# A two-layer decoder trunk on one core: who sends the mixers' turned pieces, and when a few tied steps run

## The chip, the cores and the metric

The kernel runs on one core of one Trainium2 chip. A core has four engines that compute, each with its own stream of instructions in a fixed order: TensorE (PE in the profile, its weight loads PEld), VectorE (DVE), ScalarE (ACT) and GpSimd (POOL). SyncE (SP) only issues transfers. ScalarE and GpSimd issue transfers too. All transfers of the core run on 16 DMA engines, whoever issued them; an instruction waits for others through semaphores.

The metric is the time of the whole program on the device in microseconds (us), the median of several runs. The profile is one further execution, with every instruction and DMA packet recorded.

## The reference, cut to what matters

The input is one sequence of 256 positions with 2048 features, all float32. Two layers are applied to it:

```
h = rms_norm(x);  x = x + mixer(h);  h = rms_norm(x);  x = x + conv_ffn(h)
layer 0: mixer_ab (projection 2048 -> 6144 = u,v,q,f,i,g of 1024; output projection 2048 -> 2048)
layer 1: mixer_c  (projection 2048 -> 8208 = q,k,v,g of 2048 and 16 gate columns; output 2048 -> 2048)

mixer_ab, part A: u, v = gelu(u), gelu(v);  v = rms_norm(v) per head
                  mixed[t] = sum_s tril(sp_w)[t, s] v[s] + sp_b       # 8 heads, chunks of 128
                  y_a = u * mixed
          part B: f = lb + (1 - lb) sigmoid(f);  k = (1 - lb) sigmoid(-f_logit)
                  state = f * state + k v;  o = q state               # 8 heads, gated recurrence
                  y_b = rms_norm(o) * silu(g)
mixer_c: q, k = rms_norm per head;  c = cumsum(log_sigmoid(f + b_f))
         p = softmax(q k / sqrt(128) + c[t] - c[s], causal);  y = (p v) * sigmoid(g)     # 16 heads
conv_ffn: z = h @ w_up (2048 -> 11264); causal width-3 convolution; (silu(a) * b) @ w_down (5632 -> 2048)
```

`lb` comes from a softmax over `hgrn_gamma`; `1 - lb` is called the gate floor's complement here, `omlb` in the code.

## The kernel before, in words

**Weights.** Nearly all of the time is matrix products with weights that are read once from memory. A weight tile is 128 x 1024 float32 (512 KB), fetched by SyncE (`weights`, L196). Each product is made of three matmuls in a reduced format: ScalarE copies the tile to its high part `wh` (L207), VectorE subtracts to get the low part `wl` (L212), and TensorE multiplies wh and wl with the high part of the activations and wh with their low part (L268 to L270 with the tokens' columns in 512-wide blocks, L288 to L290 in blocks of four heads). One tile feeds 12 matmuls. There are four buffers for a fetched tile and three for each part, so ScalarE and VectorE can be up to three tiles ahead of TensorE.

**Steps.** Everything else is written as Python generators that are advanced once per weight tile: `tick()` is called just before each tile is fetched, and `after(n, g)` starts a generator n ticks later. That sets where an instruction stands in its engine's stream. `LAG` is 6 and `LAST` is 7. A helper can tie an instruction behind the latest weight work that was handed over: `sum_in` and `behind(..., "sub")` put a VectorE instruction behind the latest wl subtraction, `act_in` and `copy_in` a ScalarE instruction behind the latest wh copy, `mm_in` a matmul behind the latest of the main products. Instructions that are not tied are placed by the scheduler of the framework, which may put them earlier. `project_pair` runs two column blocks of an output projection in turns: 12 of 16 row tiles of the first, 8 of the second, then the rest of each.

**Turning.** A projection in the mixers leaves a piece of 128 x 1024 elements with tokens on the partitions; what follows wants features there. `transposed` (L305 to L316) has VectorE transpose 32 x 32 blocks into `tmp` (L308) and then issues 16 transfers of 32 KB that put the blocks in place (L314). Unless a caller says otherwise they alternate between SyncE and GpSimd, eight each, so SyncE's share stands in the same queue as the weight fetches. SyncE's transfers wait for `tmp` and hold up whatever is behind them there. The mixers turn 28 pieces: 12 in mixer AB and 16 in mixer C. Their readers stand `LAG` ticks later: `add_four` adds a piece of an output projection to the residual `x` (L159, by `sum_in`) and feeds the next norm, `gates` and `queries` read the f and q pieces of mixer AB, `gated` and `spatial` its g and u pieces, `attend` the q and k pieces of mixer C, and `gate` its g pieces. Both FFNs turn their pieces in the same way, in `four` and `add_y`.

**The start of mixer AB.** ScalarE's queue fetches constants late: the identity and masks, the spatial weights `wt[0]`, their bias `wt[1]`, the convolution's columns and the levels' masks `kst`. VectorE casts `kst` to `msk` (L480) and masks `wt[0]` (L481) untied, right where the fetches are issued in the program. `values` squares and sums the eight heads' v (L353 and L354 in `sumsq`), takes the reciprocal root and scales v (L498); `mix` multiplies them with the masked weights. Both run in `mixes`, six ticks after the v projection. Then `omlb`, 8 columns of 128 features, is written to a buffer `od` in device memory feature by feature (L543, by GpSimd) and read back on all partitions as `orow` (L544), which scales the keys (L676).

**The start of mixer C.** The forget gate's 16 columns ride along in `keys_gate`. `forget` makes the running sums `fc`, writes them to device memory (`cd`, L813) and fetches them on all partitions in four loads of four heads, 512 KB each (`rows`, L791, GpSimd), at ticks 0, 4, 8 and 12 behind. `attend` reads the tile `cb` so filled in L839 and L841, four heads per load.

Of the kernel before, what the change touches and what calls it, by code (L numbers as in the profile page):

```python
# [8 lines left out]
F32 = mybir.dt.float32  # L9
# [6 lines left out]
P = 128  # L16
# [38 lines left out]
def tile_trunk(ctx: ExitStack, tc: tile.TileContext, x, pp_d, cst_d, mlev_d, msk_d,  # L55
# [87 lines left out]
    def after(n, g):  # L143
        soon.append([n, g])
# [160 lines left out]
    def transposed(src, tmp, dst, queues=None):  # L305

        for T in range(2):
            V.transpose(tmp.rearrange("p (b m i t) -> p b m i t", b=4, m=4, t=2)[:, :, :, :, T],  # L308
                        src(T).rearrange("p (m b j) -> p b m j", m=4, b=4))
        n = 2 * BLK  # L310
        for a in range(4):
            for b in range(4):
                qs = queues or (nc.sync, nc.gpsimd)
                qs[(a + b) % len(qs)].dma_start(dst[BLK * b:BLK * (b + 1), :, a * n:(a + 1) * n],  # L314
                                  tmp[BLK * a:BLK * (a + 1), b * 4 * n:(b + 1) * 4 * n]
                                  .rearrange("p (m r) -> p m r", m=4))  # L316
# [83 lines left out]
    def add_four(q, ps, z, tmp, dst, nxt):  # L400
        for T in range(2):
            SC.activation(z[:, T], ps[T], AF.Copy)
        transposed(lambda T: z[:, T], tmp, dst)

        def rest():
            for i in range(4):
                m = 4 * q + i
                sum_in(xT[m], xT[m], dst[:, i], ALU.add)
                nxt.feed(m)
                if q < 3 or i % 2:  # L410
                    yield
            if q == 3:
                for _ in range(WAIT):
                    yield
                yield from nxt.finish_tok()

        after(LAST if q == 3 else LAG, rest())


    def mixer_ab(norm):  # L420
# [45 lines left out]
        def fetch_late(*args):  # L466
# [6 lines left out]
              for _ in range(2)]  # L473
# [3 lines left out]
        msk = hp.tile([P, NL * P], BF16, tag="msk", name="msk")  # L477
        kst = hp.tile([P, NL * P], F32, tag="smk", name="kst", bufs=1)
        fetch_late(kst, msk_d)
        V.tensor_copy(msk, kst)  # L480
        V.tensor_tensor(wt[0], wt[0], cst[:, K_TRI:K_TRI + P].unsqueeze(1)  # L481
                        .to_broadcast([P, NH, P]), ALU.mult)

        ss = hp.tile([P, LANE], F32, tag="ss", name="ss")

        def values():
            for g in range(2):
                for T in range(2):
                    i = (2 * g + T) * 4
                    j = hp.tile([P, 512], F32, tag="smk", name=nm("junk"), bufs=1)  # L490
                    sumsq(ss[:, i:i + 4], gv[g][:, T], j)
                    yield
            rsq(ss[:, 0:2 * NH], ss[:, 0:2 * NH], P)
            for g in range(2):
                for T in range(2):
                    i = (2 * g + T) * 4
                    v4 = gv[g][:, T].rearrange("p (h d) -> p h d", d=P)
                    V.tensor_tensor(v4, v4, ss[:, i:i + 4].unsqueeze(2).to_broadcast([P, 4, P]), ALU.mult)  # L498
                yield

        mg = [keep("mg") for _ in range(NH)]
# [16 lines left out]
                mix(h)  # L518
                yield

        after(6, mixes())


        gam = pp[:, C_GAM:C_GAM + 3 * NH]
# [15 lines left out]
        V.tensor_scalar(lb, lb, 2.0 ** -63, None, ALU.max)  # L540
        od = dp.tile([NH, P], F32, tag="od", name="od")
        orow = hp.tile([P, NH * P], F32, tag="orow", name="orow")
        nc.gpsimd.dma_start(od.rearrange("h p -> p h"), omlb)  # L543
        nc.gpsimd.dma_start(orow.rearrange("p (h d) -> p h d", d=P), od.partition_broadcast(P))  # L544
        dgc = hp.tile([P, LANE], F32, tag="dgc", name="dgc")[:, 0:2 * NH].rearrange("p (h t) -> p h t", t=2)

# [175 lines left out]
        def spatial(j, z):  # L722
            while left[0] or j and yB[4 * j - 1] is None:
                yield
            act_in(z, z, AF.Gelu)
            for i in range(4):
                b = 4 * j + i
                m = mg[b].rearrange("p (t n) -> p t n", t=2)
                V.tensor_tensor(m, m, natural(z[:, i]), ALU.mult)
                yB[b] = quad("ya")  # L730
                split(yB[b], mg[b], turn=True)
                yield
# [17 lines left out]
    def mixer_c(norm):  # L750
# [37 lines left out]
        cb = hp.tile([P, CH * S], F32, tag="big", name="cb").rearrange("p (h s) -> p h s", s=S)  # L788

        def rows(to, of):  # L790
            nc.gpsimd.dma_start(to, of)  # L791
            yield

        def forget():
            f, fa, fc, on = (hp.tile([P, S], F32, tag=t, name=t)[0:CH] for t in ("f", "fa", "fc", "on"))
            ft = hp.tile([P, 2, LANE], F32, tag="ft", name="ft")
            V.memset(on, 1.0)
            for T in range(2):
                SC.activation(ft[:, T, 0:CH], pa[T][:, 0:CH], AF.Copy, scale=Rt[:, T:T + 1])
            yield  # L800
            ps = bank()
            for T in range(2):
                turn_in(ps[0:CH, T * P:(T + 1) * P], ft[:, T, 0:CH], ident)
            behind(V.tensor_scalar(f, ps[0:CH, 0:S], pp[0:CH, C_BF:C_BF + 1], None, ALU.add), "sub")
            yield
            copy_in(fa, f, AF.Abs)
            act(fa, fa, AF.Exp, scale=-1.0)
            act(fa, fa, AF.Ln, bias=one1[0:CH])
            yield
            V.scalar_tensor_tensor(f, f, 0.0, fa, ALU.min, ALU.subtract)  # L810
            V.tensor_tensor_scan(fc, on, f, 0.0, ALU.mult, ALU.add)
            cd = dp.tile([CH, S], F32, tag="cd", name="cd")
            nc.gpsimd.dma_start(cd, fc)  # L813
            for g in range(4):
                c = slice(4 * g, 4 * g + 4)
                after(4 * g, rows(cb[:, c], cd[c].partition_broadcast(P)))
            yield
            ps = bank()
            for T in range(2):
                turn_in(ps[:, T * CH:(T + 1) * CH], fc[:, T * P:(T + 1) * P], ident[0:CH, 0:CH])  # L820
            V.tensor_copy(ct, ps[:, 0:2 * CH].rearrange("p (t c) -> p t c", t=2))
# [104 lines left out]
        def gate(q, z):  # L926
            while left[0] or gone[0] < q:
                yield
            for T in range(2):
                act(z[:, T], z[:, T], AF.Sigmoid)  # L930
                V.tensor_tensor(z[:, T], z[:, T], os_[q][:, T], ALU.mult)
            yield
            t = piece("turn", 4)
            transposed(lambda T: z[:, T], flat(piece("tmp", 2)), heads(t))
            gone[0] += 1
            for _ in range(LAG):
                yield
            for i in range(4):
                if not room:
                    tag, n = ("big", 8) if not yB else ("o", 2)  # L940
                    w = hp.tile([P, n * 512], F32R, tag=tag, name=nm("yc"), bufs=1 if n > 2 else CH // 4)
                    room.extend(w[:, c * 512:(c + 1) * 512] for c in range(n))
                y = room.pop(0)
                src = view(heads(t)[:, i], 0, (2, 2), (1, 2), (4, P // 2))
                h, lo = (y[:, i_ * S:(i_ + 1) * S].rearrange("p (t u n) -> p t u n", t=2, u=2) for i_ in range(2))
                copy_in(h, src, AF.Copy)
                V.tensor_tensor(lo, src, h.bitcast(F32), ALU.subtract)
                yB.append(y)
                yield

        gone = [0]
        for q in range(CH // 4):
# [12 lines left out]
    def ffn(l, norm, last):  # L965
# [11 lines left out]
        def four(j0, ps=None):  # L977
            ps = ps or project_four(w_up[l, j0:j0 + 4], A, KT)
            tmp, zt = room()

            def empty():
                while norm.Rt is None:
                    yield
                z = [hp.tile([P, 512], F32, tag="z", name=nm("z"), bufs=2) for _ in range(2)]
                for T in range(2):
                    SC.activation(z[T], ps[T], AF.Copy, scale=norm.Rt[:, T:T + 1])  # L986
                transposed(lambda T: z[T], tmp, zt)
                for _ in range(LAG):
                    yield

            return zt, empty()
# [44 lines left out]
        def add_y(q, finish):  # L1036
            tmp, zt = room()
            end = last and finish and q == 2
            transposed(lambda T: y[:, T, q * 512:(q + 1) * 512], tmp, zt,
                       (nc.sync, SC, nc.gpsimd) if end else None)  # L1040

            def rest():
                for i in range(4):
                    m = 4 * q + i
                    r = sum_in(xT[m], xT[m], zt[:, i], ALU.add)
                    if end:
                        deep["early"] = r
                        tc.add_manual_dep(r.ins, deep["sum"].ins.name, order, reason="after an earlier sum")
                    if finish:
                        finish_x(m)  # L1050
                    if (q < 3 or i % 2) and not end:
                        yield
                if q == 3 and not last:
                    for _ in range(WAIT):
                        yield
                    yield from nxt.finish_tok()

            after(2 if end else LAST if q == 3 else LAG, rest())
# [148 lines left out]
```

## Time and profile before

| | us |
|---|---|
| three runs | 2301.01, 2301.51, 2304.57 |
| median | 2301.51 |
| the profiled execution | 2308.89 |
| its span, first to last instruction | 2307.1 |
| TensorE busy | 2289.0 (99%) |
| VectorE busy | 1559.8 (68%) |
| ScalarE busy | 1313.3 (57%) |
| GpSimd busy | 358.3 (16%) |

The span has these stages: mixer AB up to about 400, the first FFN to about 1130, mixer C to about 1580 and the second FFN to the end. 434.85 MB were read from HBM. The queue of SyncE and ScalarE moved 451.97 MB, GpSimd's 23.69 MB.

A row of a timeline has the start in us from the first instruction, the duration, engine, line, operation, out<-in with shapes, and in brackets the idle time of the engine just before it with what ended it. A row of issues has what was moved, who issued it, how often, its size and the median time from issue to landing. Because TensorE is nearly always busy, the rows to look for are those in which it was not.

### The profile page before, as it was taken

What the parts mean: (1) busy time and instruction counts of PE and PEld (TensorE: products, weight loads), DVE (VectorE), ACT (ScalarE), POOL (GpSimd) and SP (SyncE); (2) the same over time, 40 slices, a digit from 0 to 9 for tenths busy, and PEclk for the clock granted to TensorE, in tenths of its full rate; (3) what the DMA queues carried; (4) which work ended last, traced back from release to release, by engine and by line L of the source; (5) the groups of instructions that cost most, each with busy time, mean ns of one, the idle gap of its engine ahead of it and who ended that gap; (6) DMA issues with size and microseconds to landing.
All of it is one profiled execution on the core that took longest, in us unless ns stands there. A gap on an engine that the chain in (4) does not pass through costs nothing.

```text
span 2307.1 us, 31430 instructions
## 1 busy us (share of the span) xinstructions
PE 2289.0 (99%) x10370; PEld 1899.5 (82%) x10370; DVE 1559.8 (68%) x2369; ACT 1313.3 (57%) x1955; POOL 358.3 (16%) x664
## 2 busy tenths in 40 slices
PE   9999999999999999999999999999999999999999
PEld 7788888888888888888878888878888888888887
DVE  7788767777566657766766665667776467667666
ACT  7577655665455546654555555655655456456543
POOL 0100212122012002111311101121221022012102
PEclk9999999999999999999999999999999999999999
DMA  7756677787667767776676656767777677667765
GB/s 272 198 181 181 174 223 224 223 243 214 201 206 218 212 190 222 222 214 185 180 231 192 193 182 178 224 204 233 233 221 214 195 204 226 204 203 220 219 206 174
DMA packets 499636, 481.06 MB, mean 209 GB/s; under 512 B 117040, under 2 KB 468416, under 8 KB 499472
## 3 DMA queue, kind: packets, MB, share of 16 engines
q1 hardware_dynamic: 475488, 451.97, 64.3%
q0 software_dynamic: 21680, 23.69, 4.5%
q10 hardware_dynamic: 2304, 3.39, 0.4%
q8 instruction: 81, 1.33, 0.2%
q14 instruction: 83, 0.68, 0.1%
HBM read 434.85 MB, written 2.12 MB: 189 GB/s over the span
## 4 chain that ended last, share of the span: by engine, by line
PE 91%; DMA 4%; DVE 2%; ACT 2%; issue 1%; SPq 1%; POOL 0%; DVEq 0%; ACTq 0%
PE pm L289 26%; PE pm L290 25%; PE pm L288 25%; PE pm L269 4%; PE pm L270 4%; PE pm L268 4%; PE px L162 1%; DVE wl L212 1%; ACT wh L207 1%; DMA w<-in_w_cqkv 1%; DMA w<-in_w_abo 1%; DMA w<-in_w_f 1%; DMA w<-in_w_v 0%; DMA w<-in_w_co 0%; SPq L314 0%
## 5 line engine op out<-in xcount | busy, mean ns | idle before, releaser
L212 DVE TENSOR_TENSOR wl<-w,wh 128x1024 fp32r<-128x1024 f32 (+1 forms) x812 | 985.8, 1218 | 653.2 <-ACT wh L207 649.0
L207 ACT ACTIVATE wh<-w 128x1024 fp32r<-128x1024 f32 (+1 forms) x812 | 854.2, 1054 | 798.1 <-PE pm L290 563.2
L289 PE MATMUL pm<-wl,a 128*128 128x512 f32 x1792 | 697.9, 389 | 3.1 <-DVE wl L212 3.1
L288 PE MATMUL pm<-wh,a 128*128 128x512 f32 x1792 | 700.1, 391 | 0.7 <-ACT wh L207 0.7
L290 PE MATMUL pm<-wh,a 128*128 128x512 f32 x1792 | 697.5, 389 | 0.0
L314 POOL DMA_DIRECT2D zt<-tmp x413 | 223.7, 549 | 1201.8 <-DVE tmp L308 993.9
L289 PEld LDWEIGHTS pm<-wl,a 128*128 128x128 f32 x1792 | 336.5, 188 | 74.1 <-DVE wl L212 5.1
L288 PEld LDWEIGHTS pm<-wh,a 128*128 128x128 f32 x1792 | 336.5, 188 | 70.4 <-ACT wh L207 1.1
L290 PEld LDWEIGHTS pm<-wh,a 128*128 128x128 f32 x1792 | 336.3, 188 | 70.1
L288 PE MATMUL pm<-wh,hid 128*128 128x512 f32 x688 | 267.6, 389 | 0.0
L289 PE MATMUL pm<-wl,hid 128*128 128x512 f32 x688 | 267.6, 389 | 0.0
L290 PE MATMUL pm<-wh,hid 128*128 128x512 f32 x688 | 267.6, 389 | 0.0
L314 POOL DMA_DIRECT2D turn<-tmp x224 | 121.5, 550 | 634.1 <-DVE tmp L308 267.4
L268 PE MATMUL pm<-wh,a 128*128 128x512 f32 x464 | 183.8, 398 | 2.0 <-ACT wh L207 2.0
L269 PE MATMUL pm<-wl,a 128*128 128x512 f32 x464 | 182.2, 393 | 3.0 <-DVE wl L212 3.0
L270 PE MATMUL pm<-wh,a 128*128 128x512 f32 x464 | 181.7, 392 | 0.0
L288 PEld LDWEIGHTS pm<-wh,hid 128*128 128x128 f32 x688 | 129.1, 188 | 26.9
L289 PEld LDWEIGHTS pm<-wl,hid 128*128 128x128 f32 x688 | 129.1, 188 | 26.8
L290 PEld LDWEIGHTS pm<-wh,hid 128*128 128x128 f32 x688 | 129.1, 188 | 26.8
L269 PEld LDWEIGHTS pm<-wl,a 128*128 128x128 f32 x464 | 87.7, 189 | 23.1 <-DVE wl L212 5.7
L308 DVE STREAM_TRANSPOSE tmp<-z 128x512 f32<-128x512 f32 x132 | 92.3, 706 | 20.1 <-ACT z L986 18.1
L156 ACT ACTIVATE conv<-zt,pp 128x256 f32<-128x256 f32 x176 | 95.3, 588 | 17.4 <-DMA zt<-tmp 13.0
(217 smaller groups left out, 1928.0 us busy)
## 6 DMA issues: line engine op xcount, KB each, us to landing
w<-in_w_up SPq DMA_DIRECT2D x352, 512.0 KB, 4.5
w<-in_w_dn SPq DMA_DIRECT2D x176, 512.0 KB, 4.3
w<-in_w_cqkv SPq DMA_DIRECT2D x88, 512.0 KB, 4.4
w<-in_w_abo SPq DMA_DIRECT2D x32, 512.0 KB, 4.6
w<-in_w_cg SPq DMA_DIRECT2D x32, 512.0 KB, 4.4
w<-in_w_co SPq DMA_DIRECT2D x32, 512.0 KB, 4.6
zt<-tmp SPq DMA_DIRECT2D x414, 32.0 KB, 2.6
zt<-tmp POOLq DMA_DIRECT2D x413, 32.0 KB, 2.5
```

Source lines behind the costliest of these rows:

```text
L156: return behind(SC.activation(*args, **kw), "act")
L162: return behind(PE.matmul(*args, **kw), "main")
L207: deep["act"] = SC.activation(wh[:, p], w[:, p], AF.Copy)
L212: deep["sub"] = V.tensor_tensor(wl[:, p], w[:, p], wh[:, p].bitcast(F32), ALU.subtract)
L268: PE.matmul(ps[T], ah, h, start=k + i == 0, stop=False)
L269: PE.matmul(ps[T], ah, l, start=False, stop=False)
L270: deep["main"] = PE.matmul(ps[T], al, h, start=False, stop=k + i == KT - 1)
L288: PE.matmul(ps[T], ah, h, start=k + i == 0, stop=False)
L289: PE.matmul(ps[T], ah, l, start=False, stop=False)
L290: deep["mm"] = deep["main"] = PE.matmul(ps[T], al, h, start=False, stop=k + i == n - 1)
L308: V.transpose(tmp.rearrange("p (b m i t) -> p b m i t", b=4, m=4, t=2)[:, :, :, :, T], src(T).rearrange("p (m b j) -> p b m j", m=4, b=4))
L314: qs[(a + b) % len(qs)].dma_start(dst[BLK * b:BLK * (b + 1), :, a * n:(a + 1) * n], tmp[BLK * a:BLK * (a + 1), b * 4 * n:(b + 1) * 4 * n] ...
```

## The change

Six groups of edits:

- `transposed` sends three of four transfers by GpSimd and one by SyncE when the caller names no queues; `four` and `add_y` of the FFNs now name SyncE and GpSimd in turn, as they had it.
- `add_four` waits two ticks more for the first two of four pieces. In `gate` the last of the four pieces waits one tick less, and its four tiles go two to a tick.
- The cast of `msk`, the masking of `wt[0]`, the squares and the scaling of `values` are tied behind the wl subtraction of their tick; `mixes` starts at four ticks in place of six, and has two more steps for the first two.
- `omlb` is transposed on VectorE in 32 x 32 blocks (of a tile `ot`) and written to `od` in four transfers of 8 rows with 32 contiguous elements each.
- The products `u * mixed` in `spatial` are tied (`sum_in`).
- The four row loads of the forget gate are at ticks 5, 13, 21 and 29, each behind a memset of one column that is tied to the tick's wl subtraction.

```diff
@@ transposed
-                qs = queues or (nc.sync, nc.gpsimd)
+                qs = queues or (nc.gpsimd, nc.gpsimd, nc.gpsimd, nc.sync)
                 qs[(a + b) % len(qs)].dma_start(dst[BLK * b:BLK * (b + 1), :, a * n:(a + 1) * n],
...
@@ add_four
-        after(LAST if q == 3 else LAG, rest())
+        after(LAST if q == 3 else LAG + 2 if q < 2 else LAG, rest())
@@ mixer_ab
-        V.tensor_copy(msk, kst)
-        V.tensor_tensor(wt[0], wt[0], cst[:, K_TRI:K_TRI + P].unsqueeze(1)
-                        .to_broadcast([P, NH, P]), ALU.mult)
...
         def values():
+            behind(V.tensor_copy(msk, kst), "sub")
+            yield
+            sum_in(wt[0], wt[0], cst[:, K_TRI:K_TRI + P].unsqueeze(1).to_broadcast([P, NH, P]), ALU.mult)
+            yield
             for g in range(2):
                 for T in range(2):
...
-                    sumsq(ss[:, i:i + 4], gv[g][:, T], j)
+                    sum_in(j, gv[g][:, T], gv[g][:, T], ALU.mult)
+                    V.tensor_reduce(ss[:, i:i + 4], j.rearrange("p (h d) -> p h d", d=P), AX.X, ALU.add)
                     yield
...
-                    V.tensor_tensor(v4, v4, ss[:, i:i + 4].unsqueeze(2).to_broadcast([P, 4, P]), ALU.mult)
+                    sum_in(v4, v4, ss[:, i:i + 4].unsqueeze(2).to_broadcast([P, 4, P]), ALU.mult)
...
-        after(6, mixes())
+        after(4, mixes())
...
-        nc.gpsimd.dma_start(od.rearrange("h p -> p h"), omlb)
+        ot = hp.tile([P, LANE], F32, tag="ot", name="ot")
+        V.transpose(ot[:, 0:BLK], gm[:, 3 * NH:3 * NH + BLK])
+        for b in range(4):
+            nc.gpsimd.dma_start(od[:, b * BLK:(b + 1) * BLK], ot[b * BLK:b * BLK + NH, 0:BLK])
         nc.gpsimd.dma_start(orow.rearrange("p (h d) -> p h d", d=P), od.partition_broadcast(P))
...
@@ spatial
-                V.tensor_tensor(m, m, natural(z[:, i]), ALU.mult)
+                sum_in(m, m, natural(z[:, i]), ALU.mult)
@@ mixer_c
         def rows(to, of):
+            behind(V.memset(to[:, 0, 0:1], 0.0), "sub")
             nc.gpsimd.dma_start(to, of)
             yield
...
-                after(4 * g, rows(cb[:, c], cd[c].partition_broadcast(P)))
+                after(5 + 8 * g, rows(cb[:, c], cd[c].partition_broadcast(P)))
@@ gate
-            for _ in range(LAG):
+            for _ in range(LAG - (q == 3)):
                 yield
...
-                yield
+                if q < 3 or i % 2:
+                    yield
@@ ffn: four, add_y
-                transposed(lambda T: z[T], tmp, zt)
+                transposed(lambda T: z[T], tmp, zt, (nc.sync, nc.gpsimd))
...
-                       (nc.sync, SC, nc.gpsimd) if end else None)
+                       (nc.sync, SC, nc.gpsimd) if end else (nc.sync, nc.gpsimd))
```

## The prediction

> **What bounds the kernel.** I read the page first, then busy time by stretch, then every row of TensorE with idle time in front of it, then the queue that ends each of those waits.
>
> ```profile
> span 2307.1 us, 31430 instructions
> PE 2289.0 (99%) x10370; PEld 1899.5 (82%) x10370; DVE 1559.8 (68%) x2369; ACT 1313.3 (57%) x1955; POOL 358.3 (16%) x664
> ```
>
> TensorE is the bound, and the change removes no matmul. All it can win is TensorE's idle time, 2307.1 - 2289.0 = 18.1 us, and what follows from idle time. The stretches (columns: stretch, its length, busy us of PE, PEld, DVE, ACT, POOL, granted clock, DMA share, GB/s) say where it lies:
>
> ```profile
> 0.00:70.00 70.00, 65.03 (x281) 52.34 (x282) 48.79 (x87) 44.85 (x71) 1.25 (x5) 1.00 0.80 247
> 70.00:142.00 72.00, 70.55 (x334) 58.70 (x333) 54.27 (x120) 47.61 (x84) 9.31 (x17) 1.00 0.72 213
> 365.00:1140.00 775.00, 775.00 (x3467) 643.57 (x3467) 522.28 (x718) 429.05 (x578) 127.84 (x236) 1.00 0.71 211
> 1140.00:1190.00 50.00, 45.84 (x237) 38.35 (x236) 31.93 (x51) 24.18 (x39) 13.62 (x25) 0.97 0.81 247
> 1530.00:1570.00 40.00, 37.97 (x159) 30.54 (x158) 26.69 (x41) 22.26 (x33) 11.37 (x21) 0.96 0.69 192
> 1181.00:1186.00 5.00, 4.47 (x14) 3.34 (x13) 2.66 (x3) 2.24 (x4) 0.00 (x0) 0.66 1.00 410
> 1553.00:1558.00 5.00, 4.91 (x14) 3.87 (x15) 4.87 (x10) 3.36 (x7) 0.00 (x0) 0.66 0.89 265
> ```
>
> The first FFN (365 to 1140) has none: 775.00 busy of 775.00. The start of the trunk, the start of mixer C and its output projection have it, and in two of these places the granted clock falls to 0.66 over 5 us right behind a wait: (1 - 0.66) x 5 = 1.7 us of matmul time lost on top, each. The waits one by one, in brackets the idle time before the row and what ended it:
>
> ```profile
> 35.13 0.50 PE L269 MATMUL pm<-wl,a 128*128 128x512 f32 x1 [0.77 <-DVE wl L212]
> 53.42 0.50 PE L289 MATMUL pm<-wl,a 128*128 128x512 f32 x1 [0.88 <-DVE wl L212]
> 59.56 0.50 PE L289 MATMUL pm<-wl,a 128*128 128x512 f32 x1 [0.40 <-DVE wl L212]
> 73.95 0.49 PE L288 MATMUL pm<-wh,a 128*128 128x512 f32 x1 [0.68 <-ACT wh L207]
> 75.21 0.50 PE L289 MATMUL pm<-wl,a 128*128 128x512 f32 x1 [0.77 <-DVE wl L212]
> 266.28 0.50 PE L289 MATMUL pm<-wl,a 128*128 128x512 f32 x1 [1.03 <-DVE wl L212]
> 361.92 0.50 PE L289 MATMUL pm<-wl,yb 128*128 128x512 f32 x1 [0.37 <-DVE wl L212]
> 1165.09 0.50 PE L269 MATMUL pm<-wl,a 128*128 128x512 f32 x1 [0.97 <-DVE wl L212]
> 1180.55 0.73 PE L268 MATMUL pm<-wh,a 128*128 128x512 f32 x2 [2.03 <-ACT wh L207]
> 1181.81 0.79 PE L269 MATMUL pm<-wl,a 128*128 128x512 f32 x1 [0.53 <-DVE wl L212]
> 1551.83 0.50 PE L288 MATMUL pm<-wh,yc 128*128 128x512 f32 x1 [1.28 <-ACT wh L207]
> 1553.09 0.50 PE L289 MATMUL pm<-wl,yc 128*128 128x512 f32 x1 [0.76 <-DVE wl L212]
> ```
>
> **The change part by part.** The order of TensorE's instructions in the changed program is that of before but for two exchanged places in mixer C, so each part is priced by the wait it touches.
>
> *Masking and values tied later (L480, L481, values).* The next rows are VectorE's and ScalarE's, and two transfers in the stretch 60.7 to 73 with one of all w_f loads before 120 (KB each, median us to landing):
>
> ```profile
> 32.38 1.23 DVE L481 TENSOR_TENSOR wt<-wt,cst 128x1024 f32<-128x1024 f32 x1 [2.70 <-DMA wt<-in_spw]
> 46.79 0.63 DVE L480 CAST msk<-kst 128x896 bf16<-128x896 f32 x1 [3.25 <-DMA kst<-in_msk]
> 50.02 0.69 DVE L353 TENSOR_TENSOR junk<-gv 128x512 f32<-128x512 f32 x1 [0.95 <-ACT gv L102]
> 72.84 1.06 ACT L207 ACTIVATE wh<-w 128x1024 fp32r<-128x1024 f32 x1 [6.63 <-DMA w<-in_w_f]
> w<-in_w_f SPq DMA_DIRECT2D x1, 512.0 KB, 12.0
> od<-gm POOLq DMA_DIRECT2D x1, 4.0 KB, 11.8
> w<-in_w_f SPq DMA_DIRECT2D x12, 512.0 KB, 4.9
> ```
>
> VectorE runs in order. Before, L481 holds it 2.70 + 1.23 us for a transfer of ScalarE's queue, L480 another 3.25 + 0.63, and the sums of squares sit between the wl subtractions that TensorE awaits at 35.13, 53.42 and 59.56. All of it is moved behind later wl's: 0.77 + 0.88 + 0.40 = 2.05 us gained. The work itself stays, about 1.23 + 0.63 + 4 x 2 x 0.69 = 7.4 us, at most 1.4 us behind one wl of 1.23: 2.6 us for a weight tile. A tile feeds 12 matmuls, 12 x 775 / 3467 = 2.7 us, so it just fits. I cost it at nothing; without that cover up to 7.4 us would show. `after(4)` plus two added yields keeps the eight mix steps where they stood.
>
> *Gate floor turned by VectorE.* `od` went out as 128 x 8 single elements: 4 KB took 11.8 us, and a w_f load issued just ahead of it took 12.0 instead of 4.9, which ScalarE waits out for 6.63 us. The change writes it as four transfers of 8 rows by 32 contiguous elements after one 128x32 transpose. How long those land is unknown: between the fastest 32 KB transfer below (1.7) and 11.8; I take 2.0, the median of a turned piece's transfers, also short runs of up to 256 bytes. The waits of 73.95 and 75.21 go: 1.45 us. At 11.8 they would stay. POOL issues four instead of one, in front of the first turned piece, where it is idle.
>
> *Four of 16 transfers on SyncE, twelve on POOL (28 pieces of the mixers), sums two steps later, gate rows eight steps apart.* First mixer C's start (SP's rows; then transfers in 1164 to 1183), then its output projection:
>
> ```profile
> 1165.78 7.10 SPq L314 DMA_DIRECT2D turn<-tmp  x8
> 1174.73 2.23 SPq L196 DMA_DIRECT2D w<-in_w_cqkv  x4
> cb<-cd POOLq DMA_DIRECT2D x4, 512.0 KB, 7.4
> w<-in_w_cqkv SPq DMA_DIRECT2D x6, 512.0 KB, 7.3
> ```
> ```profile
> 1527.40 5.11 SPq L314 DMA_DIRECT2D turn<-tmp  x8
> 1540.12 0.43 DVE L159 TENSOR_TENSOR x<-x,turn 128x256 f32<-128x256 f32 x1 [2.99 <-DMA w<-in_w_co]
> 1541.20 5.10 SPq L314 DMA_DIRECT2D turn<-tmp  x8
> 1546.41 13.85 SPq L196 DMA_DIRECT2D w<-in_w_co  x8
> ```
>
> SP also fetches the weights. At 1165.78 it sends eight pieces' transfers for 7.10 us while four gate-row loads of 512 KB go out, and the next weights leave only at 1174.73 and take 7.3 us: TensorE waits 2.03 + 0.53, and 0.97 before. Now the rows go out at steps 5, 13, 21 and 29, one load per eight tiles (21 us), SP issues two more weights before that piece, and the piece holds it half as long. At 1540.12 VectorE waits 2.99 us for a late piece before it may finish the next transpose; SP stands behind that until 1541.20, then spends 5.10 us, and w_co leaves at 1546.41. With sums at LAG + 2 both transposes precede the sum, and SP's part is 4 x 0.6: the load leaves over 2.5 us earlier, more than the 1.28 + 0.76 waited. Gains: 0.97 + 2.03 + 0.53 = 3.53 and 2.04, plus 1.7 each for the clock; at 361.92, the same edge of mixer AB, 0.37. Together 9.34.
>
> The ties add a wait: a gate-row load stands on POOL until its memset, which stands behind a wl of VectorE. Queued behind it on POOL is the next piece. In the changed order the first two rows follow the k piece and precede the second group's q piece, whose projection ends at step 16, after step 13 of the second row; the third follows that piece. So nothing stands behind a waiting row; if it did, the piece would be late by up to eight tiles and its heads with it. The reader of the first row comes eight wl's after it, 21 us against 7.4 for the load.
>
> The price: a piece's slowest queue.
>
> ```profile
> L314 POOL DMA_DIRECT2D turn<-tmp x224: 548/549/619, 80.4 to 1590.4; - x112
> L314 SPq DMA_DIRECT2D turn<-tmp x224: 585/600/1763, 80.1 to 1590.9; - x112
> DMA to landing us min/median/max: 1.7/2.0/9.0
> 88.16 0.43 ACT L102 ACTIVATE kq<-turn 128x256 f32<-128x256 f32 x1 [0.90 <-DMA turn<-tmp]
> ```
>
> POOL needs 12 x 0.549 = 6.6 us where SP needed 5.1, so a piece lands 1.5 us later. Readers stand six steps (16 us) behind, and in the changed order most of them stand one weight tile (2.7 us) later still, kq of 88.16 among them. Behind a late piece the in-order ScalarE or VectorE holds back its next wh or wl; they run up to three tiles ahead. Between nothing and 28 x 1.5 = 42 us; I take 2, two new waits of the size of 266.28's, since only few readers wait today and 0.90 is such a wait without idle TensorE.
>
> *The rest.* Four memsets and the transpose, at most 4 x 0.15 + 0.7 us on a VectorE idle for a third of the time: nothing. The tied gMLP products: around 266.28 VectorE's order is unchanged, so that 1.03 stays. Last gate pieces in pairs, one step sooner: two copies beside one wl stay under a tile.
>
> **Sum.** 2.05 + 1.45 + 9.34 = 12.84 gained, 2 given back: 10.8. The profiled execution took 2308.9 us (span 2307.1 and 1.8 around it), so 2298.1 under the profiler. The median of the runs is 7.4 below that execution; the same gain puts it at 2301.5 - 10.8 = 2290.7.
>
> [...]
>
> **Rivals.** *Idle time that moves or that only the profiler has.* The timed runs are 7.4 us shorter; if that is these same waits, only 12.8 - 7.4 = 5.4 can be won, less 2: 2298.1. For it: three of the places are loads that crowd one another. Against: SP's held issues and the od scatter do not depend on being observed. *The late piece decides (slower).* If POOL's 1.5 us reaches TensorE at 12 or more of the 28 pieces, 18 us lost exceed 12.8 by the measurable 4.6: 2306.7; at all 28, 2330.7. For it: 88.16 already waits. Against: six steps, and the readers moved back. [...]
>
> **How the numbers follow.** Within 0.2% (4.6 us) is about what a measurement here cannot tell from no change: 2296.9 to 2306.1. Forecast 0.60 (its own range 2286 to 2296), all faster; idle that moves 0.22, of it 0.08 faster and 0.14 the same; late piece 0.12, of it 0.11 slower; the clock 0.06, faster. Faster 0.74, same 0.15, slower 0.11. The range is 2285 to 2304: at the low end no new wait and 3 us more from matmuls that start slowly behind a wait, at the top the moved idle time with some late pieces.
>
> **What would show it.** In the profile after: no idle row near 35, 53 and 59; w_f in the first 70 us landing in about 5 us and ScalarE's 6.63 gone; no gate-row burst, the clock at 1.00 at both places; SP's piece at x4 in 2.4 us. Wrong would be: new rows of TensorE waiting for wh or wl right behind a reader of `turn`, or waits of 1 us at 75 to 90 where the values now stand.

## The result and the profile after

The changed kernel takes 2293.95 us (median, 2292.40 to 2294.66), the kernel before beside it 2301.26 (2299.49 to 2304.57). The ratio is 0.9965, with a 95% interval of 0.9952 to 0.9978: 7.3 us faster by the medians, between 5.1 and 11.0 by the interval. The forecast was 10.8 us and 2290.7. In a later job the changed kernel took 2293.25 and the kernel before 2304.13: 10.9 us by the medians, ratio 0.9958 (0.9945 to 0.9970, which is 6.9 to 12.7 us). So 10.8 lies inside both intervals. The changed kernel is nearly the same everywhere. The kernel before moves with the chip and the run: its medians were 2301.26, 2304.23, 2304.13 and 2306.62, and its single runs went from 2298.66 to 2313.32, while the twelve of the changed kernel went from 2292.40 to 2294.92. Two of the eleven runs of the scatter kernel below took 2859 and 5984 us and are left out of its ratio.

The head of the page of the profile after, span and busy time:

```profile
span 2292.5 us, 31357 instructions
PE 2284.6 (100%) x10370; PEld 1899.8 (83%) x10370; DVE 1561.7 (68%) x2374; ACT 1314.6 (57%) x1955; POOL 420.3 (18%) x779
```

The span is 14.6 us shorter than in the profile of before. TensorE's idle time fell from 18.1 to 2292.5 - 2284.6 = 7.9 us, which is 10.2. Its busy time fell from 2289.0 to 2284.6, 4.4 us for the same matmuls; the two stretches of half clock are 3.4 of that, and the rest is not placed. The timed gain is only half of the profiled one, which the first experiment is about.

The stretches that the prediction showed, after (same columns):

```profile
0.00:70.00 70.00, 67.39 (x287) 55.40 (x288) 49.35 (x86) 47.32 (x73) 3.42 (x9) 1.00 0.80 272
70.00:142.00 72.00, 72.00 (x344) 60.41 (x343) 58.38 (x130) 48.14 (x89) 13.10 (x24) 1.00 0.63 195
1140.00:1190.00 50.00, 49.64 (x259) 42.34 (x258) 33.51 (x49) 27.14 (x41) 15.73 (x29) 1.00 0.80 243
1530.00:1570.00 40.00, 40.00 (x178) 33.11 (x177) 31.14 (x51) 25.77 (x42) 11.53 (x22) 1.00 0.70 212
```

TensorE is full from 70 to 142 and from 1530 to 1570, the clock is 1.00 in all of them. What is left of its waits (who waited for whom, us in total, times, longest):

```profile
...
PE pm L289 <- DVE wl L212: 1.0, 1, 1.0
PE pm L269 <- DVE wl L212: 0.9, 2, 0.7
...
```

There are two waits at the start (1.1 and 0.8), the wait near 266 that the prediction left standing (1.0), two of 0.3 and 0.4 behind small sums, and one wait of 0.72 at 32.99, which is that of 35.13 again. In a second profile of the changed kernel it is absent. In this profile no wait stands behind a reader that waited for a turned piece's transfers; in the second one stands there, as its section shows.

The transfers of the first 70 us that the scatter had slowed, and SyncE's queue at mixer C's start (start, duration):

```profile
w<-in_w_f SPq DMA_DIRECT2D x8, 512.0 KB, 4.7
od<-ot POOLq DMA_DIRECT2D x4, 1.0 KB, 2.6
```
```profile
1163.17 2.53 SPq L314 DMA_DIRECT2D turn<-tmp  x4
1165.80 23.71 SPq L196 DMA_DIRECT2D w<-in_w_cqkv  x10
```

`od` lands in 2.6 us (2.0 was taken, 1.7 to 11.8 the bounds), w_f in 4.7. SyncE's share of the first turned piece holds its queue for 2.53 us in place of 7.10, and ten weight loads follow at once. GpSimd's transfers of turned pieces got slower to land, in the median (before, then after):

```profile
turn<-tmp POOLq DMA_DIRECT2D x224, 32.0 KB, 1.9
turn<-tmp POOLq DMA_DIRECT2D x336, 32.0 KB, 4.0
```

By these medians that is 2.1 us on top of the 1.5 by which the prediction had a piece land later.

### The profile page after: what moved, and what is told of

It reads as the page before. It is cut to its first block, busy times and chain, and to the rows that moved or that the text cites. A ratio compares the mean times of both kernels' runs of the same rounds, so it can differ in the third digit from the quotient of the medians.

```text
span 2292.5 us, 31357 instructions
## 1 busy us (share of the span) xinstructions
PE 2284.6 (100%) x10370; PEld 1899.8 (83%) x10370; DVE 1561.7 (68%) x2374; ACT 1314.6 (57%) x1955; POOL 420.3 (18%) x779
## 4 chain that ended last, share of the span: by engine, by line
PE 96%; DVE 1%; ACT 1%; DMA 1%; issue 0%; POOL 0%; SPq 0%; DVEq 0%; ACTq 0%
PE pm L290 27%; PE pm L289 27%; PE pm L288 27%; PE pm L269 4%; PE pm L268 4%; PE pm L270 4%; PE px L162 1%; PE pm L259 1%; DVE wl L212 0%; ACT wh L207 0%; DMA w<-in_w_cqkv 0%; DMA pp<-in_pp 0%; PE px L165 0%; PE pm L233 0%; ACT L98 0%
## 5 line engine op out<-in xcount | busy, mean ns | idle before, releaser
L314 POOL DMA_DIRECT2D zt<-tmp x413 | 223.6, 549 | 1199.4 <-DVE tmp L308 983.1
L314 POOL DMA_DIRECT2D turn<-tmp x336 | 182.0, 550 | 557.0 <-DVE tmp L308 315.7
```

## The experiments

Kernels of one job share the runs of the kernel before. Where a kernel is set against the changed one, that stands at 2293.25 to 2293.95 us, ratio 0.9958 to 0.9965.

**The kernel before, once more.** No edit. The profiled gain is twice the timed one; is the first profile a fair sample?

> The kernel before, unchanged, profiled a second time. Theory (its first profiled execution, 2308.9 us, was a slow sample; some of its waits and its two half-clock stretches are not in every execution): the new profiled execution takes 2300 to 2304 us, TensorE's idle time is 9 to 14 us in place of 18.1, and at least one of the two half-clock stretches (1181, 1553) is missing; the waits at 74 and 75 us (od scatter) are there again. Rival (the profile is typical and the profiler adds some 7 us to any execution): 2307 to 2310 us again, the same dozen waits within 0.2 us each, both half-clock stretches. Timed against the kernel before: ratio 1.000.

2302.55 us, ratio 0.9993 (0.9984 to 1.0002). Its profiled execution took 2302.36 us, 6.5 less than the first one, with a span of 2300.6. TensorE's waits in the places of the prediction:

```profile
52.78 0.50 PE L289 MATMUL pm<-wl,a 128*128 128x512 f32 x1 [0.19 <-DVE wl L212]
58.91 0.50 PE L289 MATMUL pm<-wl,a 128*128 128x512 f32 x1 [0.39 <-DVE wl L212]
73.10 0.50 PE L288 MATMUL pm<-wh,a 128*128 128x512 f32 x1 [0.53 <-ACT wh L207]
74.36 0.50 PE L289 MATMUL pm<-wl,a 128*128 128x512 f32 x1 [0.76 <-DVE wl L212]
1163.66 0.50 PE L269 MATMUL pm<-wl,a 128*128 128x512 f32 x1 [0.99 <-DVE wl L212]
1178.06 0.73 PE L268 MATMUL pm<-wh,a 128*128 128x512 f32 x2 [0.93 <-ACT wh L207]
1179.31 0.50 PE L269 MATMUL pm<-wl,a 128*128 128x512 f32 x1 [0.53 <-DVE wl L212]
1182.10 0.49 PE L268 MATMUL pm<-wh,a 128*128 128x512 f32 x1 [0.22 <-ACT wh L207]
1183.37 0.50 PE L269 MATMUL pm<-wl,a 128*128 128x512 f32 x1 [0.77 <-DVE wl L212]
```
```profile
1176.00:1186.00 10.00, 7.55 (x30) 5.04 (x30) 4.85 (x4) 5.30 (x6) 0.00 (x0) 1.00 0.94 354
1530.00:1570.00 40.00, 40.00 (x177) 32.81 (x176) 28.65 (x44) 23.73 (x37) 10.58 (x20) 1.00 0.75 221
```

Three places are there again: mixer C's start with 0.99 + 0.93 + 0.53 + 0.22 + 0.77 = 3.44 (3.53 in the first profile), the scatter with 1.29 (1.45), the values with 0.58 (1.28 without the wait of 35.13). Not there again are the waits of 35.13 and 361.92, the output projection's 2.04 us, and both stretches of half clock. Of the 12.84 us that the prediction summed, 5.3 are in this execution. So part of the sum belonged to one slow execution, and the timed gain lies between the two.

The half clock is more frequent than these two profiles say. Each timed run lists its mean granted clock to three decimals, and one stretch that loses 1.7 us of 2301 makes it 0.9993, which shows as 0.999. Of the 62 runs of the kernel before that list it, 36 are at 0.997 to 0.999, among them 18 of the 19 of the last job. Of the 38 runs of the kernels that have both the turned floor and the split of 12 and 4, all are at 1.000.

**The scatter put back.** In the changed kernel:

```diff
-        ot = hp.tile([P, LANE], F32, tag="ot", name="ot")
-        V.transpose(ot[:, 0:BLK], gm[:, 3 * NH:3 * NH + BLK])
-        for b in range(4):
-            nc.gpsimd.dma_start(od[:, b * BLK:(b + 1) * BLK], ot[b * BLK:b * BLK + NH, 0:BLK])
+        nc.gpsimd.dma_start(od.rearrange("h p -> p h"), omlb)
```

> The changed kernel with the gate floor written to od element by element again, everything else as changed. Theory (the scatter's 1024 single elements hold the DMA engines for 12 us and make the weights late): od lands in about 12 us, w_f and w_q loads beside it take 10 to 12 us, TensorE waits 1.0 to 1.5 us near 70 us, and nowhere else anew; 2295 to 2296 us. Rival (the other moved work of that stretch had freed enough slack that the late weights no longer reach TensorE): the loads are as late, but no wait, and the time is that of the changed kernel, 2294 us.

2300.77 us, ratio 0.9985 (0.9976 to 0.9994): 0.0020 to 0.0027 of 2301 us worse than the changed kernel, 4.6 to 6.2 us, and 6.8 to 7.5 by the medians. Three views of this kernel: the two waits, all transfers of 55 to 70 us (packets, then issues with KB and median us to landing), and the stretch behind.

```profile
70.43 0.49 PE L288 MATMUL pm<-wh,a 128*128 128x512 f32 x1 [2.22 <-ACT wh L207]
71.69 0.79 PE L289 MATMUL pm<-wl,a 128*128 128x512 f32 x1 [0.77 <-DVE wl L212]
```
```profile
DMA packets 1212, 1.18 MB, mean 79 GB/s; under 512 B 65, under 2 KB 1212, under 8 KB 1212
...
w<-in_w_f SPq DMA_DIRECT2D x2, 512.0 KB, 13.4
w<-in_w_q SPq DMA_DIRECT2D x2, 512.0 KB, 14.0
...
od<-gm POOLq DMA_DIRECT2D x1, 4.0 KB, 10.1
```
```profile
70.00:76.00 6.00, 4.81 (x13) 3.64 (x14) 5.43 (x7) 2.49 (x3) 0.00 (x0) 0.72 1.01 355
```

The changed kernel in the same 15 us:

```profile
DMA packets 3092, 3.32 MB, mean 222 GB/s; under 512 B 236, under 2 KB 2964, under 8 KB 3092
```

While 4 KB are scattered, all of the core's transfers together move 79 GB/s in place of 222, and two loads each of w_f and w_q take 13 to 14 us. TensorE waits 2.22 + 0.77 and then runs at a clock of 0.72 for 6 us, (1 - 0.72) x 6 = 1.7: 4.7 us in all. All nine runs in the ratio list a clock of 0.998 or 0.999. The expectation had the slow loads right and the price wrong: it gave 1.0 to 1.5 us of waits and 2295 to 2296 us. The prediction's 1.45 was a third of what the trace shows here.

**Eight and eight.** In the changed kernel:

```diff
-                qs = queues or (nc.gpsimd, nc.gpsimd, nc.gpsimd, nc.sync)
+                qs = queues or (nc.sync, nc.gpsimd)
```

> The changed kernel with each turned piece split eight and eight between SyncE and GpSimd again. Theory (SyncE's share in front of the weight fetches is what made them late at the output projections and at mixer C's start): SyncE holds 5.1 us per piece, waits of 0.5 to 2.5 us return behind it at about 360 and 1545 us, and the time is 2296 to 2299 us. Rival (the later sums and the spread gate rows carry those gains alone, and the split only moves issue time): no wait over 0.5 us returns, 2293 to 2295 us.

2297.15 us, ratio 0.9969 (0.9956 to 0.9981): 0.9 to 2.5 us worse by the ratios, whose intervals overlap, and 3.2 to 3.9 by the medians; all five runs lie above all twelve of the changed kernel.

```profile
1160.29 0.50 PE L269 MATMUL pm<-wl,a 128*128 128x512 f32 x1 [1.08 <-DVE wl L212]
1174.11 0.73 PE L268 MATMUL pm<-wh,a 128*128 128x512 f32 x2 [0.37 <-ACT wh L207]
1175.37 0.50 PE L269 MATMUL pm<-wl,a 128*128 128x512 f32 x1 [0.53 <-DVE wl L212]
1178.65 0.50 PE L269 MATMUL pm<-wl,a 128*128 128x512 f32 x1 [0.50 <-DVE wl L212]
```

The waits come back at mixer C's start, 2.48 us, although the gate rows are spread. Nothing comes back at 362 or at 1550, where the expectation had the waits; only its time was met. So the shorter share on SyncE decides mixer C's start, and nothing else that this profile shows.

**The gate rows in a burst.** In the changed kernel:

```diff
-            behind(V.memset(to[:, 0, 0:1], 0.0), "sub")
...
-                after(5 + 8 * g, rows(cb[:, c], cd[c].partition_broadcast(P)))
+                after(4 * g, rows(cb[:, c], cd[c].partition_broadcast(P)))
```

> The changed kernel with the gate-row loads at steps 0, 4, 8 and 12 and without their memsets. Theory (four extra loads of 512 KB within some 18 us crowd out the weights at mixer C's start): the rows go out in pairs, w_cqkv loads beside them take 7 us, and TensorE waits 1.5 to 3 us near 1165 to 1185 us, with or without a half-clock stretch behind; 2296 to 2299 us. Rival (SyncE's shorter share alone gets the weights out in time): loads as slow, but less than 0.7 us of waits there, 2294 to 2295 us.

2294.82 us, ratio 0.9957 (0.9944 to 0.9969). In 1140 to 1190 one wait of TensorE above 0.3 us is left, 0.71 at 1149.86, behind the forget gate and not a weight. That the burst was half of the trouble falls: with SyncE's share at four, four loads of 512 KB close together cost nothing that shows in this profile.

**The changed kernel once more**, beside the next three.

> The changed kernel once more, beside the runs of this job, as what they are compared with. If the gain belongs to the two programs, the ratio to the kernel before is 0.9965 within 0.001 again. If part of it belongs to the chip, it lies outside. In its profile the stretch of 5 to 10 us may or may not show half a clock; the timed runs cannot tell.

2293.25 us, ratio 0.9958 (0.9945 to 0.9970), span 2292.8. This profile has what the prediction named as a sign of being wrong: ScalarE waits 3.40 us for a late turned piece before `gate` may read it, its next wh and VectorE's next wl come later, and TensorE waits.

```profile
1500.73 2.30 ACT L156 ACTIVATE yc<-turn 128x256 fp32r<-128x256 f32 x4 [3.40 <-DMA turn<-tmp]
1505.29 0.50 PE L289 MATMUL pm<-wl,yc 128*128 128x512 f32 x1 [0.66 <-DVE wl L212]
```

In the first profile the same reader waits 2.13 us, and nothing reaches TensorE. There readers wait for turned pieces at eight places, in the kernel before at two (0.9 and 0.7 us); the work that ScalarE and VectorE have in hand hides all but this one of 3.40.

**Masks and values untied.** In the changed kernel the cast, the masking, the squares and the scaling stand as before the change:

```diff
         def values():
-            behind(V.tensor_copy(msk, kst), "sub")
-            yield
-            sum_in(wt[0], wt[0], cst[:, K_TRI:K_TRI + P].unsqueeze(1).to_broadcast([P, NH, P]), ALU.mult)
-            yield
...
-        after(4, mixes())
+        after(6, mixes())
```

> The changed kernel with the masks and the sums of squares of the values where they stood before (not tied, mixing from step 6). My theory: VectorE holds back wl again, with TensorE waits near 52 and 58 us as in both profiles of the kernel before (0.88 and 0.40 in the first of them), perhaps 0.77 near 35: 1.3 to 2.0 us more than the changed kernel, ratio 0.9971 to 0.9974 if that one stands at 0.9965. Rival: the 52 and 58 us waits came from w_f loads slowed by the scatter and the crowd around it, which the changed kernel no longer has; then nothing changes, ratio 0.9965.

2293.98 us, ratio 0.9960 (0.9946 to 0.9973): 0.7 us from the changed kernel beside it, within the spread. Up to 80 us one wait returns:

```profile
57.34 0.50 PE L289 MATMUL pm<-wl,a 128*128 128x512 f32 x1 [0.30 <-DVE wl L212]
```

The ties bring 0.3 us here and not 2.05. The rival was nearer: that part of those waits went with other edits. Which of them took the rest was not separated; the turned floor alone (below) leaves no wait above 0.3 us between 30 and 80 us either.

**The sums back at LAG.** In the changed kernel:

```diff
-        after(LAST if q == 3 else LAG + 2 if q < 2 else LAG, rest())
+        after(LAST if q == 3 else LAG, rest())
```

> The changed kernel with the sums of the first two output pieces back at LAG instead of LAG + 2. The prediction's step: the second transpose is held again by a late piece, so SyncE's share goes out later and w_co with it, 1.28 + 0.76 us of TensorE waits at 1545 to 1555 and at most 1.7 us of half clock: 2.0 to 3.7 us more, ratio up by 0.0009 to 0.0016. Rival: with only 4 of 16 transfers SyncE has 2.7 us in hand at this place and no wait comes back: ratio that of the changed kernel. The second execution of the kernel before had no wait there either, which speaks for the rival.

2295.18 us, ratio 0.9965 (0.9952 to 0.9979), 1.9 us above the changed kernel beside it, with ranges that overlap (2293.90 to 2296.55 against 2292.75 to 2294.92). VectorE's and TensorE's rows:

```profile
355.14 0.76 DVE L159 TENSOR_TENSOR x<-x,turn 128x256 f32<-128x256 f32 x2 [2.60 <-DMA turn<-tmp]
377.80 0.76 DVE L159 TENSOR_TENSOR x<-x,turn 128x256 f32<-128x256 f32 x2 [2.34 <-DMA turn<-tmp]
```
```profile
359.42 0.50 PE L289 MATMUL pm<-wl,yb 128*128 128x512 f32 x1 [0.76 <-DVE wl L212]
382.08 0.50 PE L289 MATMUL pm<-wl,yb 128*128 128x512 f32 x1 [0.59 <-DVE wl L212]
```

Both expectations missed the place. Nothing happens at mixer C's output projection. At mixer AB's, VectorE waits 2.60 and 2.34 us for a late piece, holds back wl, and TensorE waits 0.76 + 0.59. This is the mechanism of the slower rival, and LAG + 2 is what keeps it away from the sums: it pays for the longer POOL queue rather than winning 2.04 us on SyncE. In the prediction's own row of 1540.12 a weight load (w_co), and not a piece, is named as what VectorE waited for.

**All sixteen on POOL.** In the changed kernel:

```diff
-                qs = queues or (nc.gpsimd, nc.gpsimd, nc.gpsimd, nc.sync)
+                qs = queues or (nc.gpsimd,)
```

> The changed kernel with all 16 transfers of a mixer's piece on POOL, none on SyncE: SyncE loses 28 x 4 issues of 0.6 us, a piece lands 4 x 0.549 = 2.2 us later than in the changed kernel. It doubles (and more) the price that the prediction put at 2 us and the slower rival at 1.5 us for each of 28 pieces. If lateness reaches TensorE at all, it does so here: at a third of the pieces or more, 9 x 2.2 = 20 us slower than the changed kernel (ratio 1.005), with new waits for wh or wl right behind a reader of a turned tile. If the slack of six steps covers it (the changed profile has no such wait), the ratio stays at 0.9965 within 0.001.

2295.16 us, ratio 0.9966 (0.9953 to 0.9979); 1.9 us above the changed kernel, overlapping again. The span is 2292.5, that of the first profile of the changed kernel. Its issues, and the waits that neither profile of the changed kernel has:

```profile
L314 POOL DMA_DIRECT2D turn<-tmp x448: 548/548/621, 74.9 to 1582.1; - x150
```
```profile
321.57 0.50 PE L289 MATMUL pm<-wl,ya 128*128 128x512 f32 x1 [0.41 <-DVE wl L212]
1391.03 1.58 PE L162 MATMUL px<-qk 128*128 128x128 f32 x8 [0.32 <-ACT qk L156]
1488.53 0.50 PE L289 MATMUL pm<-wl,yc 128*128 128x512 f32 x1 [0.47 <-DVE wl L212]
```

A piece whose transfers go out 16 x 0.548 = 8.8 us long in place of 6.6 costs TensorE three waits of 0.3 to 0.5 us, and not nine of 2.2. Readers of turned pieces wait here too: yb 3.9 us in two waits, yc 2.8 in two, kq 1.9 and qk 0.8 in one each. The 0.32 at 1391.03 is for that qk; the other two were not followed back. Six to eight steps of slack cover most of it.

**The turned floor alone, the split alone, both.** Three kernels from the one before, in one job. The turned floor is the opposite of the diff of the scatter; the split is this, with the FFNs' callers naming both queues as in the change:

```diff
-                qs = queues or (nc.sync, nc.gpsimd)
+                qs = queues or (nc.gpsimd, nc.gpsimd, nc.gpsimd, nc.sync)
```

> The kernel before with one edit: od turned by VectorE and written as four transfers. The prediction's term: 1.45 us, ratio 0.9994, no waits near 73 and 75 us and w_f landing in about 5 us in the first 70 us. My theory now, after the changed kernel with the scatter put back lost 4 to 6 us: the scatter is the largest part of the gain, 4 to 6 us, ratio 0.9974 to 0.9983, and the waits near 52 and 58 us shrink with it although nothing is tied.

> The kernel before with one edit: a mixer's piece sends 12 of its 16 transfers from POOL and 4 from SyncE. The prediction's terms, with the rows and the sums: 9.3 us, of which 3.5 to 5.2 at mixer C's start. My theory now: the waits of mixer C's start go (3.5 us in the first profile of before, about 3.7 in the second), the others were seldom there; 2.5 to 4 us gain, ratio 0.9983 to 0.9989. If the gate rows in a burst or the sums at LAG had to change too, waits stay at 1160 to 1185 us and the ratio is 0.999 or more.

> The kernel before with these two edits together and none of the ties, sums at LAG + 2, or spread rows. If the two edits are the whole change, the ratio is that of the changed kernel, 0.9958 to 0.9965, and the profile has 5 to 6 us of idle TensorE time. If the other edits together bring what the prediction gave the ties (2 us) and the sums (2 us), it stands 2 to 4 us above the changed kernel: 0.997 to 0.998.

| | us | ratio to before (2306.62) | 95% interval |
|---|---|---|---|
| turned floor alone | 2300.30 | 0.9970 | 0.9957 to 0.9983 |
| split alone | 2301.23 | 0.9977 | 0.9966 to 0.9989 |
| both | 2295.94 | 0.9951 | 0.9935 to 0.9967 |

The two gains add up within their intervals: 0.0030 + 0.0023 = 0.0053 against 0.0049 for both. By the medians they are 6.3, 5.4 and 10.7 us. The floor alone brings more than the 1.29 to 1.45 us of waits in the profiles of the kernel before; 18 of 19 runs of that kernel in this job list a clock below 1.000, against 3 of 8 with the floor turned, so part of it is the clock, and where the rest lies was not shown. The rows behind them, first of the turned floor alone, where no wait is left near 73 and 75, mixer C's start is as before, and the clock falls behind the long wait:

```profile
1174.42 0.73 PE L268 MATMUL pm<-wh,a 128*128 128x512 f32 x2 [1.80 <-ACT wh L207]
1175.68 0.80 PE L269 MATMUL pm<-wl,a 128*128 128x512 f32 x1 [0.53 <-DVE wl L212]
```
```profile
1174.00:1180.00 6.00, 5.05 (x15) 3.77 (x16) 2.45 (x2) 2.92 (x4) 0.00 (x0) 0.72 1.02 393
```

then of the split alone, where the scatter's waits stay (0.34 at 70.24 and the one below), with no wait above 0.3 us between 1155 and 1190, and where the sums at LAG now meet a late piece at mixer C's output projection too:

```profile
74.09 0.50 PE L289 MATMUL pm<-wl,a 128*128 128x512 f32 x1 [0.77 <-DVE wl L212]
1544.02 0.76 DVE L159 TENSOR_TENSOR x<-x,turn 128x256 f32<-128x256 f32 x2 [2.54 <-DMA turn<-tmp]
1548.31 0.50 PE L289 MATMUL pm<-wl,yc 128*128 128x512 f32 x1 [0.76 <-DVE wl L212]
```

and of both together, the waits at the places of the ties, of the sums and of mixer C's start:

```profile
57.81 0.50 PE L289 MATMUL pm<-wl,a 128*128 128x512 f32 x1 [0.39 <-DVE wl L212]
361.28 0.50 PE L289 MATMUL pm<-wl,yb 128*128 128x512 f32 x1 [0.62 <-DVE wl L212]
1180.60 0.50 PE L269 MATMUL pm<-wl,a 128*128 128x512 f32 x1 [0.70 <-DVE wl L212]
```

Both together stand 2.0 to 2.7 us above the changed kernel's two medians, measured in other jobs. The expectation of "2 to 4 us above" is met by the time and missed by the ratio (0.9951, not 0.997), because the kernel before was 2306.62 in this job. The three waits, 0.39 + 0.62 + 0.70 = 1.7 us, are of the size of that rest.

**Ten warm-up matmuls.** In the changed kernel:

```diff
-WARM = 7
+WARM = 10
```

> The changed kernel with ten warm-up matmuls instead of seven, a try at beating it and the control of this job. Three extra fill the 0.84 to 0.91 us in which TensorE waits for the first wh (ends at 5.25 us). If the half clock of the first ten matmuls (3.4 us in 5.25 to 9) follows that wait, it goes, and the kernel is about 2 us faster than the changed one, ratio 0.995 to 0.9956. If the clock opens a fixed time after TensorE's first work, nothing changes, ratio 0.9958 to 0.9965, or it is up to 0.5 us slower where the extra matmuls outlast the wait.

2291.97 us (2291.69 to 2292.27), ratio 0.9933 (0.9918 to 0.9948). All five runs lie below all twelve of the changed kernel, 1.3 to 2.0 us by the medians, though in another job: it is faster than both kernels. The stretch of 5 to 9 us, of the changed kernel, of the one with the sums at LAG, and of this one:

```profile
5.00:9.00 4.00, 3.75 (x9) 2.98 (x10) 3.28 (x7) 3.19 (x8) 0.00 (x0) 1.00 1.01 313
```
```profile
5.00:9.00 4.00, 3.70 (x16) 3.07 (x17) 3.21 (x7) 3.40 (x8) 0.00 (x0) 1.00 0.97 324
```
```profile
5.00:9.00 4.00, 4.00 (x19) 3.43 (x18) 3.18 (x7) 3.30 (x7) 0.00 (x0) 1.00 0.98 316
```

The wait for the first wh (0.84 us) is gone. The changed kernel did 9 matmuls where the same start does 16 in another execution, 7 x 775 / 3467 = 1.6 us. The granted clock reads 1.00 in all three stretches; that matmuls are slow shows in their rows alone, where the first four of the changed kernel take 2.07 us together, those here 1.34, and later ones 1.07. Of the 13 profiled executions with seven warm-ups, eight began so and five did not. Whether the three extra matmuls (six rows of the profile) prevent the slow beginning is left open: there is one profile with ten.

## Why the prediction was right or wrong

The direction, the order of size and the main mechanism (weight loads that TensorE awaits) were right. The total of 10.8 stands against 7.3 and 10.9 by the medians of two jobs. That it came so near is in part luck: terms that were too large made up for one that was too small.

| step of the prediction | said, us | the runs |
|---|---|---|
| masking and values tied later | 2.05 | 0.3 of waits, 0.7 timed |
| gate floor turned | 1.45 | 4.7 in the trace with the scatter put back, 4.6 to 7.5 timed; 6.3 for the floor alone |
| mixer C's start (split and rows) | 3.53 | 3.44 in the second profile of before; 2.48 comes back with the split undone, nothing with the rows undone; 5.4 timed for the split alone |
| output projection, and 361.92 | 2.04 + 0.37 | 2.04 and 0.37 seen once in two profiles; undoing the sums brings 1.35 at mixer AB, through late pieces |
| half clock | 3.4 | in one of two profiles and 36 of 62 timed runs of before, and again behind long waits with the scatter put back and with the floor alone; in none of 38 runs with floor and split |
| given back by late pieces | 2 | 0 and 0.66 in two profiles; with 2.2 us more lateness 1.9 by the medians, of which three waits show 1.2 |

*The weakest step is the sum itself.* It took the rows of one execution as the kernel's, and subtracted from the median. That execution was 7.4 us above the median, and 2.04 + 0.37 + 3.4 + 0.77 of the 12.84 us were not in the next one. The first rival, idle time that only the profiled execution has, said that 5.4 could be won; the second profile of before holds 5.3 of the summed waits. Its 2298.1 was still too high, since little was given back and the scatter cost more than its two waits.

*The gate floor* was priced by the two waits behind it. The duration in the prediction's own rows, 12.0 us for a w_f load beside a 4 KB transfer, said that the queue stood for some 7 us; in the first profile 1.45 of them reached TensorE, in the changed kernel with the scatter 2.99 did and took the clock with them. The 7 us were the upper end that the prediction did not give this term.

*The split* did what was said at mixer C's start, by the mechanism said: SyncE's queue held for 2.53 us in place of 7.10. The spreading of the gate rows, counted with it, brings nothing that the run without it shows once the split is there. In the kernel with floor and split alone, whose rows also go out in a burst, one wait of 0.70 stood there, so that a small part for the rows stays open. *The sums at LAG + 2* were given the wrong reason: they keep VectorE from holding back wl for a late piece, at mixer AB with the other edits in place and at mixer C with the split alone. *The late-piece rival* is real where that slack is missing (0.76 + 0.59, and 0.76) and at mixer C's `gate` in one profile of the changed kernel (0.66). The prediction had a piece land 1.5 us later from the longer queue; that GpSimd's transfers take 4.0 us to land in place of 1.9 was not in it. Still the slack held: more lateness did not reach 12 pieces. *A clock that falls without a wait*, at 0.06 in the chances, no run shows: in the stretches read here the granted clock was at 1.00 wherever no long wait stood, mixer C's start in the second profile of before among them, and fell only behind waits of 1.80 us (to 0.72 over 6 us), 2.03 (0.66 over 5) and 2.22 (0.72 over 6), and of 1.28 and 0.76 close together (0.66 over 5). Nor does a run show the 3 us that the low end of the range took from matmuls that start slowly behind a wait: besides the half clock, TensorE's busy time fell by 4.4 - 3.4 = 1.0 us.

Of what was to show it, w_f at 4.7, the clock, the missing burst and SyncE's piece of four (2.53 against 2.4) came as written. The wait near 35 did not go in the first profile after; it comes and goes in both kernels. And the sign of being wrong, a wait behind a reader of `turn`, came once, in the second profile.

## What to carry to other kernels

Take a second profile of an unchanged kernel before pricing its stalls: waits on transfers that crowd one another come and go (2.04 and 0.37 us here, in one profile of two), and only those that return are a term. Price a slow transfer by the delay that it puts on its neighbours (here a load of 12.0 us in place of 4.9), not by the one stall that shows behind it today (here 1.45 us). When a queue is relieved by lengthening another, look for the reader with the least slack, and give that one more.

## What was not expected of the hardware

While 1024 single elements of 4 bytes were written to device memory, all transfers of the core together moved 79 GB/s over 15 us, in place of 222 with the floor turned. Loads of another queue were slowed too: two of w_f on SyncE's queue took 13.4 us in place of 4.2. The trace lists 32 packets on GpSimd's queue for the 4 KB. The price paid by the neighbours is what these runs add.

The granted clock fell to 0.72 over 6 us, 1.7 us lost, behind single waits of 1.80 and 2.22 us (0.53 and 0.77 followed), and not behind 1.08 or behind 0.93 + 0.53. At the program's start 9 or 16 matmuls fit into the same 4 us in two of the profiles, while the granted clock reads 1.00 in both.

POOL issued 448 transfers of turned pieces, twice as many as before, with none above 621 ns. What grew was the time to land: a median of 4.0 us with twelve transfers of a piece issued there, in place of 1.9 with eight. Over all transfers of L314, those of the FFNs among them, it was 2.4 us with eight, 2.8 with twelve and 3.1 with all sixteen.
